# A one-core HGRN2/conv encoder layer: keys of six half heads made in a stage of their own and kept in DRAM

## The chip, the cores and the metric

One Trainium2 chip, one of its cores. The metric is device time in microseconds of one execution of the whole layer. Engines are named as in the profile: PE (matrix products), PEld (loading of a product's stationary operand), DVE (elementwise on vectors), ACT (activations, copies and casts), POOL, SP (which here only issues DMAs).

## The reference

One layer of a bidirectional encoder on 1024 positions x 1024 channels, float32 in and out:

```python
proj = jnp.einsum("bsd,de->bse", h, w_in)            # h = RMSNorm(x)
glu_in, q, v, z_f, z_b, og, g_a, g_b = jnp.split(proj, SPLIT_POINTS, axis=-1)
a = jax.nn.glu(glu_in, axis=-1)
a = _dwconv_centred(a, dw_w, dw_b)                   # 31 taps
a = jax.nn.silu(_layernorm(a, ln_w, ln_b))
a = jnp.einsum("bsc,cd->bsd", a, pw_w)               # the pointwise product
o = _bi_hgrn2(q, v, z_f, z_b, lb[0], lb[1])          # the scan, 8 heads of 128
of = o * lax.rsqrt(jnp.mean(o * o, axis=-1, keepdims=True) + EPS)
bmix = (of * norm_w * jax.nn.silu(og)) @ o_w
merged = jax.nn.sigmoid(g_a) * a + jax.nn.sigmoid(g_b) * bmix
...
# the scan, for each head and direction:
f = lb + (1.0 - lb) * jax.nn.sigmoid(z)              # decay, clipped to [1e-6, 1]
k = (1.0 - lb) * jax.nn.sigmoid(-z)
# S_t = diag(f_t) S_{t-1} + k_t v_t^T ,  o_t = S_t^T q_t
```

Then x += merged @ w_out, a gated FFN (up projection of 2 x 2816 columns, a 3-tap convolution on the gate, down projection), and a last RMSNorm.

## The kernel before

Activations lie with channels on the 128 partitions and positions along the row, in pages of 128x512 (a half of the positions; `H` is 512). A float32 product is made as three products of reduced operands (`mm3`, L138): an operand is split into a rounded part, an ACT cast (L121), and what is left, a subtraction on DVE or POOL (L118).

**Jobs and filler.** A job is the product of one block of 128 weight columns with all activations (`std_job`, L192), or a Strassen-like pair of blocks (`pair_job`, L224, whose weight sums are made by accumulating DMAs that POOL issues, L238). `run_jobs` (L149) prepares the weights of the next job, by an SP load into `wr`, an ACT cast and a DVE subtraction into `wp`, once the job before has begun. A job yields after every two steps of k, that is after six matmuls of 128x512: this is one unit. `Stream.fill(n)` (L172) advances a stream of jobs by n units, with the fraction carried over, so that units can be laid between other work. PE's instructions stand in the order in which the program issues them. The other engines' orders are made by the framework's scheduler from dependences and its own estimates.

**Order of the stages.** Input projection in 17 pairs, with the convolution beside it; layer norm of the convolved channels, for each half of the positions, after which the eight pointwise jobs of this half (2 units each, kept in the list `pw_jobs`) are put at the head of the list of jobs; then the scan, with 22 columns of the projection that are left over (`rest_jobs`, 176 units) as its filler stream `dense`; output projection of the scan, merge, w_out, FFN up, FFN down.

**The scan** has 16 half heads (8 heads, two halves of the positions; loop at L1011 to L1043). For half head i:

- `scan_inputs(i)` (L741) loads q and, for both directions, z, and makes on ACT the gates f and k (six activations), which DVE then clips (L762).
- `scan_base` (L765) is a generator: on DVE it makes products of decays within blocks of 8 positions (tile `DE`, with a reciprocal, L786), the block products `fm` and `tb`, the decayed queries and keys `Qh` and `Kh`, and from these `qF` and `kG`, which are what the levels start from. It yields between its instructions. One `Base` object holds the generator of the next half head, and is advanced by `step(BASE_STEPS)`, 2 yields.
- `scan_levels` (L825) makes the scores in four levels of block size 8, 16, 32 and 64. A level is an ACT copy of a part of kG to `A` (L835), four products of 128x128 (L838; the trace shows eight records), an update of kG (DVE, L730), a masked copy out of the bank (L865 to L869) and an update of qF; the next level needs both updates. The first level also has the products of Qh and Kh (L851).
- `scan_states` (L887) transposes kG (PE, L894), copies it out (`kT`, ACT, L896), multiplies by v and adds up the states `Sf` and `Sb`. The outputs of a head (L926 and L985) are made during the next head as the stream `pending`.

`between(fill)` (L1022) stands behind each of the four levels and the three steps of the states, seven times per half head: `dense.fill(FILL)` with FILL = 1.3, two steps of the next half head's keys, one step of `pending`. Before the first half head `dense.fill(21)` covers the making of its keys. Behind the last, `left` units (10) are laid between the last head's outputs and the loads of `bm` (L1001), the scan's results, which come back from DRAM for the output projection.

**Down projection.** 22 blocks of the FFN's hidden channels in groups of 4, 4, 5, 5, 4; for each group eight jobs. The pages of the next group are loaded and split (`load_g`) at once, three units into the group.

Of the kernel before, what the change touches and what calls it, by code (L numbers as in the profile page):

```python
# [10 lines left out]
F32 = mybir.dt.float32  # L11
# [5 lines left out]
AX = mybir.AxisListType  # L17

P = 128
FILL = 1.3  # L20
CONV_FILL = 1.6
NPAIRS = 17
LN_FILL = 6
# [21 lines left out]
def tile_hybrid_encoder(  # L45
# [45 lines left out]
    def nm(s):  # L91
        uid[0] += 1
        return f"{s}_{uid[0]}"
# [216 lines left out]
    ones_m = cp.tile([P, P], F32, name="ones_m")  # L310
    G.memset(ones_m, 1.0)

    gp0 = tc.alloc_tile_pool(name="gp0", bufs=1, reuse_waits="tile")
    p0 = tc.alloc_tile_pool(name="p0", bufs=1, reuse_waits="tile")
    x_in = []

# [346 lines left out]
    for half in range(2):  # L663
        xs = []
        for j in range(NCW):
            if j % 2 == 0:
                both = p1.tile([P, 2, H], F32, tag="ca", name=nm("cx"), bufs=2)
            nc.sync.dma_start(both[:, j % 2, :], d_cv[j][half])
            xs.append(both[:, j % 2, :])
        s_pairs.fill(LN_FILL)  # L670
        mean = bank("ob")
        T.matmul(mean, ones_m, total(xs, tmp()), start=True, stop=True)
        for t in xs:
            V.scalar_tensor_tensor(t, mean, -1.0 / CW, t, op0=ALU.mult, op1=ALU.add)
        s_pairs.fill(LN_FILL)
        sqs = [tmp() for _ in xs]
        for sq, t in zip(sqs, xs):
            A.activation(sq, t, AF.Square)
        rstd = rstd_over_partitions(total(sqs, sqs[0]), CW, "ob", tmp())
        next(rstd)  # L680
        s_pairs.fill(3)
        rs = next(rstd)
        ca = []
        for j, xn in enumerate(xs):
            V.tensor_tensor(xn, xn, rs, op=ALU.mult)
            V.tensor_scalar(xn, xn, vec("lnw", j), vec("lnb", j), op0=ALU.mult, op1=ALU.add)
            A.activation(xn, xn, AF.Silu)
            both = gp0.tile([P, 2, H], F32R, tag="gl", name=nm("ch"), bufs=NCW)
            ca.append(split(both[:, 0, :], both[:, 1, :], xn, V))
        s_pairs.fill(LN_LAST)  # L690
        at = 0
        while at < len(jobs) and jobs[at] in pw_jobs:
            at += 1
        for i in range(ND):
            job = std_job(
                w_cols(conv_pw_w, 0, NCW, i * P), NCW, lambda k, hf, ca=ca: ca[k], store(d_a[i]), (half,)
            )
            pw_jobs.append(job)
# [19 lines left out]
    hp = tc.alloc_tile_pool(name="heads", bufs=1, reuse_waits="tile")  # L718
    NB = H // 8
    DE = hp.tile([P, 2, 2, H], F32, name="DE")  # L720
    dg = hp.tile([P, H], F32, name="dg")
    E0, D0 = 0, 2 * H
    for o in (E0 + 3, D0 + 3):
        G.memset(view(DE, o, [[8, 2 * NB]]), 1.0)
    G.memset(dg, 0.0)

    N2 = 2 * NB

# [12 lines left out]
    def scan_inputs(i):  # L741


        h, half = divmod(i, 2)
        q = page(hp, "q", 2)
        f = hp.tile([P, 2, H], F32, tag="f", name=nm("f"), bufs=2)
        kk = hp.tile([P, 2, H], F32, tag="k", name=nm("k"), bufs=2)
        nc.sync.dma_start(q, d_q[h][half])
        for d in range(2):
            z = page(hp, "zi", 3)  # L750
# [4 lines left out]
            A.activation(  # L755
                fo,
                z.rearrange("p (b e) -> p b e", e=8),
                AF.Identity,
                scale=oml_of(d, h),
                bias=lb_of(d, h),  # L760
            )
        V.tensor_scalar(f, f, MIN_FORGET, 1.0, op0=ALU.max, op1=ALU.min)  # L762
        return q, f, kk, kscale[:, h : h + NH + 1 : NH]

    def scan_base(ins):  # L765


        q, f, kk, ks = ins

        def two(t, *r):  # L770
            if len(r) == 1:
                return view(t, r[0], [[8, N2]])
            return view(t, r[0], [[r[1] - r[0], 2], [8, N2]])

# [11 lines left out]
        V.reciprocal(ed(D, 7), ed(0, D + 7))  # L786
        yield

        fm = hp.tile([P, 2, NB], F32, tag="fm", name=nm("fm"), bufs=2)
        turned = view(fm, NB, [[-NB, 2], [1, NB]])  # L790
        tt(turned, view(f, 0, [[H, 2], [8, NB]]), view(DE, E0, [[H, 2], [8, NB]]))
        tb = hp.tile([P, 3, NB], F32, tag="tb", name=nm("tb"), bufs=3)
        tt(tb[:, 0:2, :], turned, view(DE, D + 7, [[H, 2], [8, NB]]))
        V.tensor_copy(tb[:, 2, :], tb[:, 0, :])
# [6 lines left out]
        qF = hp.tile([P, 2, H], F32, tag="qF", name=nm("qF"), bufs=3)  # L801
        kG = hp.tile([P, 2, H], F32, tag="kG", name=nm("kG"), bufs=2)
        Qh = hp.tile([P, 2, H], F32, tag="Qh", name=nm("Qh"), bufs=1)
        Kh = hp.tile([P, 2, H], F32, tag="Kh", name=nm("Kh"), bufs=1)
        along = [[8, NB], [1, 8]]
        for d in range(2):
            m0, st = ((0, 1), (7, -1))[d]
            whole = [[8, NB], [st, 8]]
            tt(view(Qh, (1 - d) * H + m0, whole), view(q, m0, whole), view(DE, D + d * H, along))
            yield  # L810
            keys(
                view(Kh, d * H + m0, whole),
                view(kk, d * H + m0, whole),
                ks[:, d : d + 1],
                view(DE, d * H, along),
            )
# [6 lines left out]
        yield qF, kG, [(Qh[:, 1 - d, :], Kh[:, d, :]) for d in range(2)], tb  # L823

    def scan_levels(base, S_t, Tt):  # L825

# [144 lines left out]

    class Base:
        def __init__(self, ins):
            self.gen, self.val = scan_base(ins), None

        def step(self, n):
            while n > 0 and self.val is None:
# [26 lines left out]
            bm[h][half] = split(hx(), hx(), load(d_bm[h][half]), V)  # L1004

    NI = 2 * NH
    cur = Base(scan_inputs(0))
    ins = scan_inputs(1)
    dense.fill(21)
    pending = Stream(iter(()))  # L1010
    for h in range(NH):  # L1011
        Tt = hp.tile([P, 2, 2, 4], F32, tag="Tt", name=nm("Tt"), bufs=3)
# [3 lines left out]
        for half in range(2):  # L1016
            i = 2 * h + half
            base = cur.result()
            ahead = Base(ins) if i + 1 < NI else None
            ins = scan_inputs(i + 2) if i + 2 < NI else None  # L1020

            def between(fill):  # L1022
                dense.fill(fill)
                if ahead is not None:
                    ahead.step(BASE_STEPS)
                pending.fill(1)

            S_t = hp.tile([P, 4, P], F32, tag="S", name=nm("S"), bufs=3)
            vl = load(d_v[h][half])
            for n, _ in enumerate(scan_levels(base, S_t, Tt[:, half])):  # L1030
                if n == 2:
                    b = bank("tr")
                    for c in range(4):
                        T.transpose(b[:, c * P : (c + 1) * P], vl[:, c * P : (c + 1) * P], ident)
                    v = hp.tile([P, 4, DK], F32, tag="v", name=nm("v"), bufs=3)
                    A.copy(v.rearrange("p c e -> p (c e)"), b)
                between(FILL)
            qF, kG = base[0], base[1]
            for _ in scan_states(i, kG, v, Tt, Sf, Sb):
                between(FILL)  # L1040
# [15 lines left out]
    bm_loads(1)  # L1056
    pending.drain()
    hp.release()


    fw = tc.alloc_tile_pool(name="fw", bufs=1, reuse_waits="tile")
# [310 lines left out]
```

## Time and profile before

| what | value |
|---|---|
| time, median of 3 runs | 1899.92 us (1898.41 to 1903.82) |
| the profiled execution | 1905.6 us, its span 1903.8 us |
| PE busy | 1799.7 us, 95% of the span |
| DVE, ACT, POOL busy | 67%, 42%, 11% |
| first level of the scan starts (PE, L838) | 561.15 us |
| first matmul of the output projection | 1011.00 us |
| q0 and q1 (the two queues with nearly all bytes), share of 16 engines | 15.2% and 41.5% |

The page has one profiled execution. A group or timeline line names line, engine, operation, output tile, input tile and shape; the bracket tells how long the engine was idle before and what ended it.

### The profile page before, as it was taken

The numbers are of one execution on the slowest core, as the hardware profiler recorded it, in microseconds if no ns is written. First come the engines' busy times: TensorE is split into PE (matmuls) and PEld (weight loads), VectorE is DVE, ScalarE is ACT, GpSimd is POOL, SyncE is SP. The second block draws the span as 40 slices with busy tenths as digits, with TensorE's granted clock in tenths as the row PEclk, the third lists the DMA queues.
The fourth block names the chain that finished last, engine by engine and source line by source line (L and its number), as shares of the span: only waits on it lengthen the run. The fifth ranks groups of instructions, "written<-read, shape, count | busy, mean of one in ns | idle before, by whom it ended". The sixth has DMA issues, their size and how long they took to land.

```text
span 1903.8 us, 23750 instructions
## 1 busy us (share of the span) xinstructions
PE 1799.7 (95%) x8543; PEld 1484.0 (78%) x8543; DVE 1270.2 (67%) x1860; ACT 799.2 (42%) x1488; POOL 210.9 (11%) x218
## 2 busy tenths in 40 slices
PE   6988999999999998999998999899999999999996
PEld 5767878887778887888786888588888888788885
DVE  3488999535469898999835555667676666534445
ACT  6433333234554554555443134544343344522124
POOL 3101111213100001000100000111111111000000
PEclk9999999999999999999998999899999999999998
DMA  7747788786563333342237665777676676733134
GB/s 256 219 119 169 179 188 199 185 182 148 190 192 89 113 108 96 111 122 82 75 95 216 197 200 183 185 153 154 147 151 143 143 156 128 221 93 96 54 89 162
DMA packets 323916, 285.09 MB, mean 150 GB/s; under 512 B 14926, under 2 KB 245078, under 8 KB 323798
## 3 DMA queue, kind: packets, MB, share of 16 engines
q1 hardware_dynamic: 272006, 242.67, 41.5%
q0 software_dynamic: 51792, 40.90, 15.2%
q8 instruction: 67, 1.10, 0.3%
q14 instruction: 51, 0.42, 0.1%
HBM read 191.24 MB, written 71.83 MB: 138 GB/s over the span
## 4 chain that ended last, share of the span: by engine, by line
PE 66%; DVE 13%; DMA 8%; ACT 6%; issue 3%; POOL 2%; SPq 0%; ACTq 0%; POOLq 0%; DVEq 0%
PE mm L143 16%; PE mm L144 16%; PE mm L145 16%; PE sc L144 3%; PE sc L145 3%; PE sc L143 3%; PE tr L143 2%; PE tr L144 2%; PE tr L145 2%; DVE wp L118 1%; DVE kG L730 1%; DVE DE L730 1%; PE sc L838 1%; DVE qF L730 1%; DMA wr<-wr 1%
## 5 line engine op out<-in xcount | busy, mean ns | idle before, releaser
L143 PE MATMUL mm<-hx,wp 128*128 128x512 f32 x1176 | 482.6, 410 | 24.6 <-ACT hx L121 8.6
L145 PE MATMUL mm<-hx,wp 128*128 128x512 f32 x1176 | 467.4, 397 | 3.9 <-DVE wp L118 3.9
L144 PE MATMUL mm<-hx,wp 128*128 128x512 f32 x1176 | 466.8, 397 | 2.9 <-POOL hx L118 1.9
L121 ACT CAST wp<-wr 128x1024 fp32r<-128x1024 f32 (+2 forms) x196 | 179.7, 917 | 323.0 <-PE mm L144 222.9
L143 PEld LDWEIGHTS mm<-hx,wp 128*128 128x128 f32 x1176 | 226.5, 193 | 73.7 <-ACT hx L121 9.5
L118 DVE TENSOR_TENSOR wp<-wr,wp 128x1024 fp32r<-128x1024 f32 (+2 forms) x196 | 206.9, 1056 | 102.9 <-ACT wp L121 97.4
L145 PEld LDWEIGHTS mm<-hx,wp 128*128 128x128 f32 x1176 | 225.5, 192 | 55.1 <-DVE wp L118 5.4
L144 PEld LDWEIGHTS mm<-hx,wp 128*128 128x128 f32 x1176 | 226.5, 193 | 48.4 <-POOL hx L118 3.6
L645 DVE SCALAR_TENSOR_TENSOR acc<-gl,v_b,acc 128x1024 f32<-128x1024 f32 x120 | 150.1, 1285 | 0.5
L143 PE MATMUL sc<-hy,wq 128*128 128x512 f32 x244 | 97.3, 399 | 3.1 <-ACT hy L121 3.0
L144 PE MATMUL sc<-hy,wq 128*128 128x512 f32 x244 | 96.7, 396 | 2.7 <-DVE hy L118 2.7
L145 PE MATMUL sc<-hy,wq 128*128 128x512 f32 x244 | 96.2, 394 | 0.0
L238 POOL DMA_DIRECT2D wr<-sw x39 | 34.9, 896 | 519.3 <-DVE wp L118 297.4
L1251 DVE TENSOR_TENSOR xr<-mm,xr 128x512 f32<-128x512 f32 x48 | 33.1, 690 | 82.0 <-PE mm L145 82.0
L838 PEld LDWEIGHTS sc<-qF,A 128*128 128x128 f32 x512 | 65.9, 193 | 19.0 <-issue 13.3
L838 PE MATMUL sc<-qF,A 128*128 128x128 f32 x512 | 69.1, 278 | 11.7 <-DVE qF L730 10.6
L121 ACT CAST wq<-sw 128x1024 fp32r<-128x1024 f32 x39 | 41.1, 1054 | 86.6 <-PE mm L144 66.4
L143 PE MATMUL mm<-hy,wp 128*128 128x512 f32 x156 | 63.2, 405 | 7.4 <-ACT wp L121 5.3
L266 ACT COPY su<-mm 128x512 f32<-128x512 f32 x78 | 45.5, 583 | 53.4 <-PE mm L145 53.4
L835 ACT COPY A<-kG 128x512 f32<-128x512 f32 x64 | 39.7, 620 | 66.3 <-DVE kG L730 37.8
L1169 DVE SCALAR_TENSOR_TENSOR tm<-gp,v_a,tm 128x512 f32<-128x512 f32 x88 | 65.6, 746 | 1.8 <-ACT tm L1165 0.9
L1153 DVE TENSOR_TENSOR ft<-su,mm 128x512 f32<-128x512 f32 x22 | 15.1, 687 | 71.6 <-issue 68.1
(281 smaller groups left out, 3548.6 us busy)
## 6 DMA issues: line engine op xcount, KB each, us to landing
wr<-in_w_in_dram SPq DMA_DIRECT2D x55, 512.0 KB, 6.5
sw<-in_ffn_w_up_dram SPq DMA_DIRECT2D x44, 256.0 KB, 3.5
sw<-in_ffn_w_up_dram POOLq DMA_DIRECT2D x22, 512.0 KB, 8.3
wr<-in_ffn_w_up_dram SPq DMA_DIRECT2D x22, 512.0 KB
d_g<-ft SPq DMA_DIRECT2D x44, 256.0 KB, 5.9
ev<-d_g SPq DMA_DIRECT2D x44, 256.0 KB, 3.2
wr<-sw POOLq DMA_DIRECT2D x39, 256.0 KB, 3.3
wr<-wr POOLq DMA_DIRECT2D x39, 256.0 KB, 3.8
```

The costliest lines, as they stand in the source:

```text
L118: eng.tensor_tensor(lo, src, hi.bitcast(F32), op=ALU.subtract)
L121: A.copy(hi, src)
L143: T.matmul(acc, whi[:, k, :], ahi, start=first, stop=False, skip_group_check=again)
L144: T.matmul(acc, whi[:, k, :], alo, start=False, stop=False, skip_group_check=again)
L145: T.matmul(acc, wlo[:, k, :], ahi, start=False, stop=last, skip_group_check=again)
L238: G.dma_start(o, a, accum_op=ALU.add)
L266: A.copy(t, acc)
L645: V.scalar_tensor_tensor(acc, g[:, k : k + S], tap(k), acc, op0=ALU.mult, op1=ALU.add)
L730: V.tensor_tensor(o, a, b, op=op)
L835: A.copy(A_t.rearrange("p (b x e) -> p b x e", x=2, e=h), pairs(kG, h))
L838: T.matmul(b[:, c * P : (c + 1) * P].rearrange("p (b x e) -> p b x e", x=2, e=h), A_t[:, c * P : (c + 1) * P], view(qF, c * P, [[2 * h, P ...
L1169: V.scalar_tensor_tensor(c, g[:, o + k : o + k + H], vec("fdw", k * NF + j), c, op0=ALU.mult, op1=ALU.add,)
```

## The change

- `EARLY = 6`. The eight pointwise jobs of the second half of the positions are no longer put at the head of the jobs ahead of the scan, but at the head of `dense`, which so has 192 units.
- A new stage stands between the projection and the scan: for half heads 0 to 5, `store_keys` makes inputs and keys (without qF and kG) into one page `Qk` of 128x2496 float32 (1.28 MB: Qh, Kh, fm, tb, and `ends`, a copy on ACT of the last decays of the blocks), and SP stores it to `d_keys[i]`. `Qk` has one buffer. At each of the nine yields of a half head one unit of `dense` is laid (54), and after the stage six more.
- In the scan, half heads 0 to 5 load their `Qk` back with one DMA and make only qF and kG (`scan_decayed`). The others make their keys as before, in the same page.
- The filler per slot is `EARLY_FILL` = 0.6 while the next half head is an early one, and FILL = 1.25 from then on. 15 units are left behind the last half head.
- The tiles of the gates lie in a pool of their own (`hb`), made before the stage, and the pool of the scan is made after it; the pool with the split convolution channels (`gp0`) is moved to the other side of the memory and lives until the keys are stored.
- In the down projection the loads and splits of the next group are spread: nine units, then one block of channels each four units.

```diff
-FILL = 1.3
+EARLY = 6
+EARLY_FILL = 0.6
+FILL = 1.25
...
+    KEYS = 4 * H + 7 * (H // 8)
+    d_keys = [dp.tile([P, KEYS], F32, name=f"d_keys_{i}") for i in range(EARLY)]
...
             pw_jobs.append(job)
-            jobs.insert(at + i, job)
+            if half == 0:
+                jobs.insert(at + i, job)
     s_pairs.drain()
     Stream(run_jobs(jobs)).drain()
     p1.release()
-    gp0.release()
...
-    dense = Stream(run_jobs(rest_jobs))
+    dense = Stream(run_jobs(pw_jobs[ND:] + rest_jobs))
...
+    def key_page():
+        t = hb.tile([P, KEYS], F32, tag="Qk", name=nm("Qk"), bufs=1)
+        Qh, Kh = t[:, 0 : 2 * H], t[:, 2 * H : 4 * H]
+        o = 4 * H
+        return t, Qh, Kh, t[:, o : o + N2], t[:, o + N2 : o + N2 + 3 * NB], t[:, o + N2 + 3 * NB :]
 
-    def scan_base(ins):
+    def scan_keys(ins, keyed):
         q, f, kk, ks = ins
+        t, Qh, Kh, fm, tb, ends = keyed
...
+    def scan_decayed(keyed, ends, along):
+        t, Qh, Kh, fm, tb, _ = keyed
+        qF = hp.tile([P, 2, H], F32, tag="qF", name=nm("qF"), bufs=3)
+        kG = hp.tile([P, 2, H], F32, tag="kG", name=nm("kG"), bufs=2)
         both = [[H, 2], [8, NB], [1, 8]]
         tt(view(qF, 0, both), view(Qh, 0, both), view(fm, 0, [[NB, 2], [1, NB], [0, 8]]))
         yield
-        tt(view(kG, 0, both), view(Kh, 0, both), view(DE, D + 7, [[H, 2], [8, NB], [0, 8]]))
+        tt(view(kG, 0, both), view(Kh, 0, both), view(ends, 0, along + [[0, 8]]))
         yield
...
+    def store_keys(i):
+        keyed = key_page()
+        yield from scan_keys(scan_inputs(i), keyed)
+        A.copy(view(keyed[5], 0, [[NB, 2], [1, NB]]), ends_of())
+        nc.sync.dma_start(d_keys[i], keyed[0])
+
+    def scan_base(i, ins):
+        keyed = key_page()
+        if i < EARLY:
+            nc.sync.dma_start(keyed[0], d_keys[i])
+            yield
+            yield
+            yield from scan_decayed(keyed, keyed[5], [[NB, 2], [1, NB]])
+        else:
+            yield from scan_keys(ins, keyed)
+            yield from scan_decayed(keyed, DE[:, 1, 0, 7:], [[H, 2], [8, NB]])
...
-    cur = Base(scan_inputs(0))
-    ins = scan_inputs(1)
-    dense.fill(21)
+    for i in range(EARLY):
+        for _ in store_keys(i):
+            dense.fill(1)
+    gp0.release()
+    hp = tc.alloc_tile_pool(name="heads", bufs=1, reuse_waits="tile")
...
+    def inputs(i):
+        return i, scan_inputs(i) if i >= EARLY else None
+
+    cur = Base(inputs(0))
+    ins = inputs(1)
+    dense.fill(6)
...
-                between(FILL)
+                between(FILL if i + 1 >= EARLY else EARLY_FILL)
...
-    left = 8 * (len(rest) - 2) + 16 - dense.count
+    left = 2 * ND + 8 * (len(rest) - 2) + 16 - dense.count
...
             if not last:
-                load_g(f0 + group, groups[n + 1])
+                st.fill(9)
+                for f in range(f0 + group, f0 + group + groups[n + 1]):
+                    load_g(f, 1)
+                    st.fill(4)
             st.drain()
```

More of the change, by code (lines that the diff above doesn't have):

```diff
@@ L311, in tile_hybrid_encoder @@
     G.memset(ones_m, 1.0)
-    gp0 = tc.alloc_tile_pool(name="gp0", bufs=1, reuse_waits="tile")
+    gp0 = tc.alloc_tile_pool(name="gp0", bufs=1, side="right", reuse_waits="tile")
     p0 = tc.alloc_tile_pool(name="p0", bufs=1, reuse_waits="tile")
@@ L714, in tile_hybrid_encoder @@
         h12.append(split(hx(), hx(), t, V))
-    dense = Stream(run_jobs(rest_jobs))
-    hp = tc.alloc_tile_pool(name="heads", bufs=1, reuse_waits="tile")
+    dense = Stream(run_jobs(pw_jobs[ND:] + rest_jobs))
+    hb = tc.alloc_tile_pool(name="gates", bufs=1, reuse_waits="tile")
     NB = H // 8
-    DE = hp.tile([P, 2, 2, H], F32, name="DE")
-    dg = hp.tile([P, H], F32, name="dg")
+    DE = hb.tile([P, 2, 2, H], F32, name="DE")
     E0, D0 = 0, 2 * H
@@ L744, in scan_inputs @@
         h, half = divmod(i, 2)
-        q = page(hp, "q", 2)
-        f = hp.tile([P, 2, H], F32, tag="f", name=nm("f"), bufs=2)
-        kk = hp.tile([P, 2, H], F32, tag="k", name=nm("k"), bufs=2)
+        q = page(hb, "q", 2)
+        f = hb.tile([P, 2, H], F32, tag="f", name=nm("f"), bufs=2)
+        kk = hb.tile([P, 2, H], F32, tag="k", name=nm("k"), bufs=2)
         nc.sync.dma_start(q, d_q[h][half])
         for d in range(2):
-            z = page(hp, "zi", 3)
+            z = page(hb, "zi", 3)
             nc.sync.dma_start(z, d_z[d][h][half])
@@ L787, in scan_base @@
         yield
-        fm = hp.tile([P, 2, NB], F32, tag="fm", name=nm("fm"), bufs=2)
         turned = view(fm, NB, [[-NB, 2], [1, NB]])
         tt(turned, view(f, 0, [[H, 2], [8, NB]]), view(DE, E0, [[H, 2], [8, NB]]))
-        tb = hp.tile([P, 3, NB], F32, tag="tb", name=nm("tb"), bufs=3)
-        tt(tb[:, 0:2, :], turned, view(DE, D + 7, [[H, 2], [8, NB]]))
-        V.tensor_copy(tb[:, 2, :], tb[:, 0, :])
+        tt(view(tb, 0, [[NB, 2], [1, NB]]), turned, view(DE, D + 7, [[H, 2], [8, NB]]))
+        V.tensor_copy(tb[:, 2 * NB :], tb[:, 0:NB])
         tt(ed(D + 1, 6), ed(D, 7), fv(1, 7))
@@ L799, in scan_base @@
         yield
[L801 to L804, printed above, removed]
         along = [[8, NB], [1, 8]]
@@ L820, in scan_base, with ends_of @@
         yield
-        tt(view(kG, 0, both), view(Kh, 0, both), view(DE, D + 7, [[H, 2], [8, NB], [0, 8]]))
+        tt(view(kG, 0, both), view(Kh, 0, both), view(ends, 0, along + [[0, 8]]))
         yield
-        yield qF, kG, [(Qh[:, 1 - d, :], Kh[:, d, :]) for d in range(2)], tb
+        qk = [(Qh[:, (1 - d) * H : (2 - d) * H], Kh[:, d * H : (d + 1) * H]) for d in range(2)]
+        yield qF, kG, qk, tb
+    def ends_of():
+        return view(DE, D0 + 7, [[H, 2], [8, NB]])
+    def store_keys(i):
[13 more added lines that the diff above has]
+            yield from scan_decayed(keyed, DE[:, 1, 0, 7:], [[H, 2], [8, NB]])
     def scan_levels(base, S_t, Tt):
@@ L973, in __init__ @@
         def __init__(self, ins):
-            self.gen, self.val = scan_base(ins), None
+            self.gen, self.val = scan_base(*ins), None
         def step(self, n):
@@ L1006, in tile_hybrid_encoder @@
     NI = 2 * NH
-    cur = Base(scan_inputs(0))
-    ins = scan_inputs(1)
-    dense.fill(21)
+    for i in range(EARLY):
[3 more added lines that the diff above has]
+    hp = tc.alloc_tile_pool(name="heads", bufs=1, reuse_waits="tile")
+    dg = hp.tile([P, H], F32, name="dg")
+    G.memset(dg, 0.0)
+    def inputs(i):
[3 more added lines that the diff above has]
+    dense.fill(6)
     pending = Stream(iter(()))
@@ L1019, in tile_hybrid_encoder @@
             ahead = Base(ins) if i + 1 < NI else None
-            ins = scan_inputs(i + 2) if i + 2 < NI else None
+            ins = inputs(i + 2) if i + 2 < NI else None
             def between(fill):
@@ L1036, in tile_hybrid_encoder @@
                     A.copy(v.rearrange("p c e -> p (c e)"), b)
-                between(FILL)
+                between(FILL if i + 1 >= EARLY else EARLY_FILL)
             qF, kG = base[0], base[1]
             for _ in scan_states(i, kG, v, Tt, Sf, Sb):
-                between(FILL)
+                between(FILL if i + 1 >= EARLY else EARLY_FILL)
             kept.append((S_t, v, qF))
@@ L1058, in tile_hybrid_encoder @@
     hp.release()
+    hb.release()
     fw = tc.alloc_tile_pool(name="fw", bufs=1, reuse_waits="tile")
```

1 line of the change is left out of this document (removed).

## The prediction

> **What bounds the kernel now.** I read the shares of the page, then the stretch around the scan as windows (columns: length, busy us and instructions of PE, weight load, DVE, ACT, POOL; granted clock, DMA share, GB/s): two parts of the projection ahead of the scan, half heads 0 to 5, half heads 6 to 15, and the way into the output projection.
>
> ```profile
> PE 1799.7 (95%) x8543; PEld 1484.0 (78%) x8543; DVE 1270.2 (67%) x1860; ACT 799.2 (42%) x1488; POOL 210.9 (11%) x218
> ```
>
> ```profile
> 507.90:532.50 24.60, 23.19 (x97) 18.04 (x97) 8.57 (x12) 10.83 (x19) 0.00 (x0) 1.00 0.67 202
> 532.50:561.10 28.60, 28.60 (x127) 23.62 (x126) 17.82 (x28) 17.61 (x28) 1.08 (x3) 1.00 0.65 201
> 561.10:715.60 154.50, 142.43 (x885) 124.87 (x885) 143.78 (x263) 82.56 (x179) 6.77 (x8) 0.98 0.34 105
> 715.60:976.60 261.00, 244.65 (x1562) 214.56 (x1562) 225.11 (x420) 135.43 (x318) 19.97 (x20) 0.99 0.31 96
> 976.60:1016.60 40.00, 28.70 (x140) 23.43 (x139) 13.37 (x22) 17.81 (x45) 4.03 (x5) 0.86 0.49 135
> ```
>
> PE is full except in the scan and behind it, and the change leaves PE's instructions as many as they were: it can only move PE's waits. At full rate a 512-wide matmul starts every 0.227 us (560.24, 560.46, 560.69) and a 128-wide one every 0.112. The first six half heads hold 324 wide and 561 narrow ones: 136.4 us of 154.5, so 18.1 are lost; the other ten 546 and 1016: 237.7 of 261.0, 23.3 lost. DVE is busy 93% of the first six. The idle time of PE from 561 to 1017, by what ended it (us, times, longest):
>
> ```profile
> PE sc L838 <- DVE qF L730: 10.6, 9, 2.8
> PE mm L143 <- ACT hx L121: 8.3, 1, 8.3
> PE tr L894 <- ACT kT L896: 7.4, 3, 2.9
> ```
>
> The second row is one gap, at the first output projection job; PE's and ACT's timelines show it (start, length, instruction, idle before it and its releaser):
>
> ```profile
> 571.74 2.05 PE L838 MATMUL sc<-qF,A 128*128 128x128 f32 x8 [2.78 <-DVE qF L730]
> ...
> 1007.43 1.04 ACT L121 CAST wq<-sw 128x1024 fp32r<-128x1024 f32 x1 [7.88 <-DMA sw<-in_ffn_w_up_dram]
> ...
> 1011.00 0.79 PE L143 MATMUL mm<-hx,wp 128*128 128x512 f32 x1 [8.27 <-ACT hx L121]
> ```
>
> ACT stands in a cast of the first FFN weight, whose transfer POOL issued at 996.66, with the hx splits behind it. Gaps of over 2.5 us are followed by slow PE: the level at 571.74 takes 2.05 us where the one at 561.15 takes 1.05, and behind a 4.61 us gap at 1644.65 twelve matmuls start 0.44 apart (a further 2.5 us).
>
> **A. The key stage and the way into the scan.** DVE's timeline prices one half head's keys:
>
> ```profile
> 544.20 0.69 DVE L762 TENSOR_SCALAR f<-f 128x1024 f32<-128x1024 f32 x1 [9.04 <-ACT f L755]
> ...
> 547.22 1.75 DVE L786 RECIPROCAL DE<-DE 128x256 f32<-128x256 f32 x1
> ...
> 555.26 0.74 DVE L733 SCALAR_TENSOR_TENSOR Kh<-k,kscale,DE 128x512 f32<-128x512 f32 x1
> 555.92 1.22 DVE L730 TENSOR_TENSOR qF<-Qh,fm 128x1024 f32<-128x1024 f32 x1
> 557.05 1.22 DVE L730 TENSOR_TENSOR kG<-Kh,DE 128x1024 f32<-128x1024 f32 x1
> ```
>
> From 544.20 to 549.78 it is 5.6, then 0.1 for a copy and 4.0 from 551.62 to 555.92 less the strips between: 9.7 us, and 2.4 more for qF and kG, which stay in the scan. PE now runs 54 filler units (6 wide matmuls, 1.36 us each) plus 6 from 507.9 on, 23 of them after where the first level starts today: with no wait the scan would begin at 561.15 + 23 x 1.36 = 592.5. DVE sets another pace. The first f is clipped near 521 (the first pointwise job is out by 515, then a table load and six activations, about 5 us). Its keys take 9.7 and four weight splits of the pointwise jobs 0.6 each: 532.7. In the order of the built program the weight cast of the first other job stands on ACT behind the copy of the ends, which waits for those keys; with cast 1.05 and subtract 1.2 it is ready at 537.1, where PE would have it at 532.3: a wait of 4.8. Half heads 1 to 5 take 9.7 + 1.2 for a split, 10.9, up to 12.5 each with the waits for f. At 12.5 the last keys are done at 595, PE's units at 597.3.
>
> Then the new round trip: Qk has one buffer, so load 0 waits for store 5. A 256 KB page is stored in 2.2 and loaded in 2.9 us (d_z and zi of the issue table), at 2048 B packets of 84 ns on 16 engines 0.7 of it transfer; 1.278 MB makes it 3.3: store 4.8, load 5.4. With the copy 0.3, issue 0.8, qF and kG 2.4 and the A copy 0.8 the first level follows the last keys by 14.5 us: 609.6, so PE, out of units at 597.3, waits 12.3. Two slow restarts of 2.5 bring the stage to 4.8 + 12.3 + 5 = 22.1. With pace 10.9 the keys end 8 us earlier (587): level at 601.6, 9.1 behind 592.5, with one restart 11.6. If nothing at all waits but the round trip, less the 7 units that stand behind the last key step (9.5), it is 14.4 - 9.5 + 2.5 = 7.4. If DMA stretches the stage (below) 34. I take the middle of 11.6 and 22.1: **+17**, bounds 7.4 and 34.
>
> The 18 loads of q and z of these half heads leave SP earlier, the 12 key transfers (15.3 MB) are new. They stand in SP's queue with the weight loads of the jobs, which run one job (10.9 us) ahead; a load held 5 us behind a store that waits for its keys is still early. The DMA engines were at 0.67 share there: this is the cover, and if it is gone the next rival's price holds. POOL gets nothing new here.
>
> **B. Half heads 0 to 5.** DVE loses 9.7 of its some 25 us in each, PE 0.7 x 7 = 4.9 filler units. What then bounds is the chain from level to level. At the end of the scan, where there is no filler, it shows itself:
>
> ```profile
> 961.00 0.74 DVE L869 COPY_PREDICATED S<-m,sc 128x512 f32<-128x512 uint8 x1 [0.49 <-PE sc L838]
> 961.65 0.66 DVE L730 TENSOR_TENSOR qF<-qF,tb 128x512 f32<-128x512 f32 x1
> ```
>
> From the last product of a level to the next level PE waits 1.7 us (a copy .74, a qF .67, latency), of which a unit covers 1.36 and transposes of v .36. With 0.6 units a slot, about every other slot has none. Walking the built PE order with these prices, the six wait 3.3, 2.1, 2.7, 2.5, 2.0 and 2.3, and the 2 to 3 clock drops of such gaps cost 0.45 each per half head: 17.6, against 18.1 lost now. **-0.5**; bounds -11 (all six lose the 1.2 of the best half heads, 10 and 11) and +6 (all like today's third, 4.7 us, with half again for the load of Qk).
>
> **C. Half heads 6 to 15.** FILL 1.25 for 1.3 takes 3.5 units (4.8 us) from a stretch where DVE bounds about half of the slots (the second of each pair of half heads waits 1.3 to 2): they come back behind the scan as PE work. **+2.4**; bounds 0 and 4.8.
>
> **D. The way out of the scan.** Today 976.6 to 1017 loses 1.4 (Sb), 0.7, 8.3, 1.0 and 2.5 of slow PE: 13.8. Five more units are left (15 for 10), 6.8 us in which the FFN weight can come; and the built order has POOL's transfer ahead of the last head's rstd and ACT's cast of it in the last half head, ahead of its kT copies. There ACT's cast waits 10.8 us from issue (996.66 to 1007.43): kT comes at 20.7 us into the half head where PE wants it at 16.0, 4.7 and a restart of 2.5. Two loads of bm at a time (988.63, 993.97, 999.42: 5.4 us a round) still cost 3. -13.8 + 4.7 + 2.5 + 3 = **-3.6**; bounds -13.8 and +3 (the cast waits as long as today, in the scan, and the bm round twice).
>
> **E. Down projection.** With the d_g loads spread one f at a time, ACT's splits stand less in front of the xr copies, which end the 4.61 gap at 1644.65: **-1.3**, a guess at one split and its share of the restart; bounds -4.5 (the gap gone) and 0, since no load moves ahead of what it fed before.
>
> Sum: 17 - 0.5 + 2.4 - 3.6 - 1.3 = +14.0. It is a difference between stretches of one execution (span 1903.8, reported 1905.6, 5.7 above the median of 1899.92), and I put it on the median: 1913.9.
>
> The slow restart by row is 2.5 us. The Trainium skill (TensorE: Matmul & The Clock Gate, Part 1: The HAM clock gate) says that an idle PE falls to half clock and needs about 3.4 us of sustained work to come back; half of 3.4 is 1.7 a restart, an estimate from that page, and with it the sum would be 1.2 lower (one or two restarts in A). The trace gives more (2.5), and I keep it.
>
> **Rivals.** Faster: the first level starts within some 5 us of the last filler unit (A 7.4), early half heads, freed of 39% of their DVE work, lose like the best (B -11), and the last half head has its FFN weight in time (D -12): 7.4 - 11 + 2.4 - 12 - 1.3 = -14.5, 1885.4. For it: DVE at 93%, and 10.6 us of waits for qF. Against: units are fewer exactly where the chain, not DVE's sum, is the wait. It decides if the levels find qF ready with 0.6 units a slot. Chance 0.22.
>
> Slower still: the stage is bound by DMA. Per half head of 11.6 us it moves a stored Qk (1.28 MB), three loaded pages (0.79) and one job's weights and stores (1.05 per 10.9 us, so 1.12): 3.19 MB, 275 GB/s; 202 at share 0.67 scales to 301, so 0.91 of what there is. Stores then take 8 us for 4.8 and, with one Qk, DVE stands 2.5 us in each of five half heads: 12 to 17 more in A, 34 in all: 1930.9. Against: the mean leaves room. Chance 0.12. The Trainium skill (DMA: Bandwidth & Descriptors, Specifications) names 358 GB/s per core from HBM; by that the stage would be at 0.77, and this rival weaker.
>
> No change: A 11.6, B -0.5, C 2.4, D -10, E -1.3: +2.2, 1902.1; for it, the tail's 8.3 us gap has a plain cause that is moved. Chance 0.13. That the change doesn't do what it says is excluded by the built order: six sets of keys and stores stand ahead of the first level, six loads behind.
>
> **How the numbers follow.** The forecast has 0.53. Its own range is 1903 to 1924 (A 11.6 to 22.1, the rest by half its bounds). 8 in 10: from 1889, cutting half of the faster case, to 1928, cutting most of the DMA case. 0.3%, 5.7 us, is what a measurement can tell: faster 0.23 (that rival, and a sliver of the third), same 0.12, slower 0.65 (forecast and DMA case).
>
> **What would show it.** A: a PE gap of some 12 us ahead of the first level, ended by DVE's qF behind a load of Qk; about 5 at the first job after the pointwise ones, ended by DVE's wp. B: half heads 0 to 5 lose some 3 us each as now. D: no 8 us gap at the output projection, and an ACT cast in the last half head that waits on sw with PE behind it for kT. Wrong would be: the first level within 5 us of the last unit, half heads 0 to 5 at under 1.5 lost, or stores of Qk over 8 us.

## The result, and the profile after

The changed kernel takes 1910.55 us (median of 20 runs, 1899.45 to 1919.86) against 1901.24 us for the kernel before beside it (20 runs, 1897.0 to 1911.81): 1.0045 of its time, 95% interval 1.003 to 1.006, so 6 to 11 us slower. In a second series (12 runs, and 34 of the kernel before) the ratio was 1.0039 (1.0025 to 1.0053). The forecast was 14 us more.

The runs of one kernel lie up to 20 us apart here. The profiled execution of the changed kernel (1899.45 us) is the fastest of its 20, and that of the kernel before (1905.6 us) one of the slower: the two pages compared as wholes would say that the change gains 6 us. So the stretches are compared, over several profiles, and the sums are checked against medians. One source of the scatter, found in e3, bears on every comparison here.

Page of the changed kernel, the engines' shares, and its windows (columns as in the prediction): the key stage, the wait behind it, half heads 0 to 5, half heads 6 to 15, the way out.

```profile
PE 1792.4 (94%) x8543; PEld 1478.2 (78%) x8543; DVE 1277.0 (67%) x1860; ACT 802.2 (42%) x1494; POOL 208.0 (11%) x218
```

```profile
532.00:592.00 60.00, 59.44 (x261) 48.73 (x261) 55.62 (x87) 32.54 (x54) 0.00 (x0) 1.00 0.84 283
592.00:605.30 13.30, 0.76 (x5) 0.30 (x3) 5.35 (x9) 2.70 (x5) 0.00 (x0) 0.68 0.79 266
605.30:727.97 122.67, 110.42 (x734) 98.56 (x735) 97.24 (x177) 58.98 (x139) 5.58 (x8) 0.97 0.35 114
727.97:981.97 254.00, 238.67 (x1538) 210.07 (x1537) 224.63 (x420) 133.91 (x316) 18.58 (x21) 0.99 0.33 100
981.97:1022.00 40.03, 38.73 (x194) 31.79 (x193) 14.27 (x23) 20.15 (x48) 2.42 (x4) 1.00 0.53 163
```

PE is full in the key stage (59.4 of 60 us, at 283 GB/s), idle for 12.5 us behind it, and full again behind the scan (38.7 of 40.0, where it was 28.7). DVE, at 93% in the first six half heads before, is at 79% there now. PE's idle time from 555 to 1017 us, by what ended it:

```profile
PE sc L871 <- ACT A L868: 12.5, 1, 12.5
PE sc L871 <- DVE qF L732: 10.4, 11, 1.5
PE tr L927 <- DVE ev L998: 8.9, 7, 2.7
```

The 8.3 us at the output projection are gone; 12.5 us at the first level have come; the waits for qF are what they were (10.6 before), though DVE has less to do. The long gap in the timelines of SP, DVE and PE:

```profile
588.80 0.38 SPq L844 DMA_DIRECT2D d_keys<-Qk  x1
594.89 0.32 SPq L850 DMA_DIRECT2D Qk<-d_keys  x1
...
602.23 1.23 DVE L732 TENSOR_TENSOR qF<-Qk 128x1024 f32<-128x1024 f32 x1 [7.85 <-DMA Qk<-d_keys]
...
605.29 2.08 PE L871 MATMUL sc<-qF,A 128*128 128x128 f32 x8 [12.54 <-ACT A L868]
```

Behind the last keys (588.54) come a store of 6 us, only then the load into the same buffer, 7.3 us to qF, then kG and A. The last filler unit has started by 592.4. The way out of the scan, ACT's and PE's timelines:

```profile
976.45 1.05 ACT L123 CAST wq<-sw 128x1024 fp32r<-128x1024 f32 x1 [6.46 <-DMA sw<-in_ffn_w_up_dram]
...
979.92 1.16 PE L936 MATMUL ob<-v,kT 128*128 128x128 f32 x8 [1.84 <-ACT kT L929]
```

ACT waits for the FFN weight in the last half head, ahead of the kT copies, and PE waits for these, but for 1.8 us.

### The profile page after: what moved, and what is told of

Same layout as the page of the kernel before. It is cut to its first block, busy times and chain, and to the rows that moved or that the text cites. A ratio compares the mean times of both kernels' runs of the same rounds, so it can differ in the third digit from the quotient of the medians.

```text
span 1897.7 us, 23788 instructions
## 1 busy us (share of the span) xinstructions
PE 1792.4 (94%) x8543; PEld 1478.2 (78%) x8543; DVE 1277.0 (67%) x1860; ACT 802.2 (42%) x1494; POOL 208.0 (11%) x218
## 4 chain that ended last, share of the span: by engine, by line
PE 59%; DVE 16%; DMA 13%; ACT 6%; issue 4%; POOL 1%; SPq 1%; ACTq 0%; POOLq 0%; DVEq 0%
PE mm L145 14%; PE mm L146 14%; PE mm L147 14%; PE sc L146 3%; PE sc L147 2%; PE sc L145 2%; DMA sw<-in_w_in_dram 2%; DMA wr<-wr 2%; DMA wr<-sw 2%; DVE DE L732 2%; DVE wp L120 2%; DMA sw<-in_ffn_w_up_dram 1%; PE sc L871 1%; DVE Qk L732 1%; DVE acc L649 1%
## 5 line engine op out<-in xcount | busy, mean ns | idle before, releaser
L145 PE MATMUL mm<-hx,wp 128*128 128x512 f32 x1176 | 476.2, 405 | 14.4 <-ACT wp L123 4.4
L147 PE MATMUL mm<-hx,wp 128*128 128x512 f32 x1176 | 463.7, 394 | 3.8 <-DVE wp L120 3.8
L146 PE MATMUL mm<-hx,wp 128*128 128x512 f32 x1176 | 462.5, 393 | 2.1 <-POOL hx L120 1.8
L145 PEld LDWEIGHTS mm<-hx,wp 128*128 128x128 f32 x1176 | 223.3, 190 | 62.7 <-DVE ev L592 5.4
L147 PEld LDWEIGHTS mm<-hx,wp 128*128 128x128 f32 x1176 | 222.7, 189 | 54.7 <-DVE wp L120 6.7
L146 PEld LDWEIGHTS mm<-hx,wp 128*128 128x128 f32 x1176 | 223.5, 190 | 47.6 <-POOL hx L120 3.6
L871 PE MATMUL sc<-qF,A 128*128 128x128 f32 x512 | 69.4, 279 | 23.0 <-ACT A L868 12.5
L123 ACT CAST wq<-sw 128x1024 fp32r<-128x1024 f32 x39 | 41.1, 1054 | 84.8 <-PE mm L146 66.9
L145 PE MATMUL mm<-hy,wp 128*128 128x512 f32 x156 | 63.2, 405 | 6.7 <-ACT wp L123 5.3
L147 PE MATMUL mm<-hy,wp 128*128 128x512 f32 x156 | 62.6, 401 | 0.0
```

Of the source, the lines that this page charges most:

```text
L123: A.copy(hi, src)
L145: T.matmul(acc, whi[:, k, :], ahi, start=first, stop=False, skip_group_check=again)
L146: T.matmul(acc, whi[:, k, :], alo, start=False, stop=False, skip_group_check=again)
L147: T.matmul(acc, wlo[:, k, :], ahi, start=False, stop=last, skip_group_check=again)
L871: T.matmul(b[:, c * P : (c + 1) * P].rearrange("p (b x e) -> p b x e", x=2, e=h), A_t[:, c * P : (c + 1) * P], view(qF, c * P, [[2 * h, P ...
```

## The experiments

Each kernel was timed in five rounds beside the kernel before, except e11. "Loss" is PE's time in a half head less its work at full rate (0.227 us for a wide, 0.112 for a narrow matmul).

**e1: the changed kernel again.** No edit.

> The changed kernel once more, to see which of its waits are the same in a second profiled execution. Theory (the sum of the prediction): the one long gap of PE ahead of the first level is 12 to 13 us again, no gap over 4 us stands between the scan and the output projection, and the time is 8 to 10 us above the kernel before. Rival (the time beyond the first profile, which came out 11 us under the median, lies in the change): some gap that the first profile doesn't have, of 5 us or more, stands in the key stage, the scan or the down projection.

1904.55 us, ratio 1.0039 (7.4 us over before). The gap ahead of the first level is 10.9 us and starts the level at 605.63 (605.29 in the first profile); no gap over 2.8 us stands between it and the output projection. Nothing new in the second profile, and yet an execution 5 us longer: the first profile was a lucky execution of the same mechanism, as the theory says, though the gap is a little under its 12 to 13.

**e2: half head 0 stays in Qk.**

```diff
-    for i in range(EARLY):
+    for i in [*range(1, EARLY), 0]:
         for _ in store_keys(i):
...
-        nc.sync.dma_start(d_keys[i], keyed[0])
+        if i:
+            nc.sync.dma_start(d_keys[i], keyed[0])
+        else:
+            in_place.append(keyed)
...
-        keyed = key_page()
+        keyed = key_page() if i else in_place.pop()
         if i < EARLY:
-            nc.sync.dma_start(keyed[0], d_keys[i])
+            if i:
+                nc.sync.dma_start(keyed[0], d_keys[i])
```

> The keys of half heads 1 to 5 are made first, those of half head 0 last; these stay in Qk and are neither stored nor loaded. All else as in the changed kernel. Theory (the first level waits for the store of the last keys and the load of the first, one behind the other on one buffer): the 12.5 us gap of PE at the first level is gone or under 2.5 us, and the time is 12 to 15 us under the changed kernel's (1896 to 1899). Rival (the stage is late because DVE's keys are late, or because DMA is full): the gap shrinks by less than half, to 6 us or more, the time by less than 6 us. Second rival: the gap moves to half head 1, whose load now waits for Qk to be free of half head 0: the levels of half head 1 start 5 us later and half of the gain is lost.

1895.65 us, ratio 0.9987 (0.997 to 1.0004); the changed kernel beside it 1904.55. PE's timeline at the first level:

```profile
593.54 0.39 PE L147 MATMUL mm<-hx,wp 128*128 128x512 f32 x1
593.76 1.05 PE L875 MATMUL sc<-qF,A 128*128 128x128 f32 x8
```

There is no gap at all, and the level starts 11.9 us earlier than in e1 (11.5 earlier than in the first profile); a 2.1 us gap opens at the second level. So the round trip is the wait. The gain, 8.9 us between the medians, is less than the 12 to 15 expected, and half head 1 is not late (2.75 lost, 2.76 before this edit), so the second rival falls.

**e3 and e4: the spread loads of the down projection.** e3 takes them out of the changed kernel, e4 puts them alone into the kernel before.

```diff
-                st.fill(9)
-                for f in range(f0 + group, f0 + group + groups[n + 1]):
-                    load_g(f, 1)
-                    st.fill(4)
+                load_g(f0 + group, groups[n + 1])
```

> The changed kernel with the loads and splits of the next group of the down projection at once, as before the change; the rest of the change stays. Theory (the spread is worth what the profiles differ by behind 1632 us, 5 us): 4 to 6 us slower than the changed kernel, 1914 to 1917, and a gap of PE over 4 us at the start of the down projection. Rival (what the prediction took, one split less ahead of the xr copies): 1 to 2 us slower.

> The kernel before with the spread loads of the down projection alone. Theory: 4 to 6 us faster than the kernel before, 1895 to 1897, the 4.6 us gap at the start of the down projection under 3 us. Rival: 1 to 2 us faster, 1899 to 1900, the gap nearly as long.

e3: 1906.78 us, ratio 1.0051 (1.0033 to 1.007), 2.2 us over e1. e4: ratio 0.9991 (0.9973 to 1.0008), about 1.7 us under before, not clear of nothing. The gap at the start of the down projection is 4.15 us in e3, 2.85 in e4. On the gap both theories came true (over 4 us, under 3), on the time their rival: what the prediction had taken (1.3) is nearer, and the 5 us between the first two profiles were scatter.

e3 also showed one place where scatter comes from. Its code differs from e1's only behind 1600 us, but its half head 12 lost 9.2 us, in e1 1.9. POOL's timeline, e3 first and then e1:

```profile
898.76 7.32 POOL L409 TENSOR_TENSOR ors<-ors,mhalf 128x4 f32<-128x4 f32 x1
```

```profile
895.35 1.01 POOL L409 TENSOR_TENSOR ors<-ors,mhalf 128x4 f32<-128x4 f32 x1
```

The same instruction, the root of four numbers per partition, takes 1.01 us in one execution and 7.32 in another. ACT's scaling of the outputs waits for it, and PE for that.

**e5 and e8: FILL alone, and with the spread loads,** in the kernel before.

```diff
-FILL = 1.3
+FILL = 1.25
```

> The kernel before with FILL 1.25 instead of 1.3 and nothing else, so that 15 units are left behind the scan. Theory (the 8 us gap at the output projection is ACT's wait for the first FFN weight, and what removes it in the changed kernel is where the cast stands and the five more units, not the keys): the gap is under 3 us, the time 6 to 10 us under the kernel before, the losses of the half heads as before. Rival (it takes the earlier place in the last half head, which only the changed kernel's order has): a gap of 5 us or more stays and the time is within 4 us of the kernel before.

> The kernel before with FILL 1.25 and the spread loads of the down projection, without early keys: the two parts of the change that should gain. Theory (parts add up): 8 to 11 us under the kernel before, and so 15 or more under the changed kernel. Rival (both stages end in a wait that takes the place of the one removed): within 4 us of the kernel before.

Ratios 1.0002 (0.9987 to 1.0018) and 1.0 (0.9981 to 1.0018): no gain. But the gap at the output projection is 1.5 us in both, where the kernel before and e4 have 8.3 and 7.5. So the theory of the tail is right, the time is not. In both, half head 4 loses 12.5 and 12.8 us, in the kernel before 2.7, and POOL's, ACT's and PE's timelines of e5 say why:

```profile
671.55 5.46 POOL L405 TENSOR_TENSOR ors<-ors,mhalf 128x4 f32<-128x4 f32 x1
...
677.04 1.28 ACT L955 ACTIVATE tm<-tm,ors 128x128 f32<-128x128 f32 x4 [6.65 <-POOL ors L405]
...
686.84 1.11 PE L894 MATMUL tr<-ident,kG 128*128 128x128 f32 x4 [6.30 <-ACT kT L896]
```

With other filler the instructions of the half heads shift against each other, and the long POOL operation turns up at another head: what the tail gained was given back there. e8 has it at the same place (5.49 us).

**e6 and e7: more filler in the early half heads,** on e2's kernel.

```diff
-EARLY_FILL = 0.6
-FILL = 1.25
+EARLY_FILL = 1.3
+FILL = 1.0
...
-    dense.fill(6)
+    dense.fill(3)
```

e7 has 1.0 and 1.1 in place of 1.3 and 1.0.

> The kernel with half head 0 in place (run before), with 1.3 filler units per slot in half heads 0 to 4, 1.0 in the later ones and 3 units for 6 ahead of the scan. Theory (with 0.6 units a slot the wait is the chain from level to level, not DVE's sum): half heads 0 to 4 lose under 8 us of PE together, where they lose 18 with 0.6; half heads 6 to 15, where DVE bounds, lose 1 to 2 us more each than with 1.25, so that the time is 0 to 8 us above the same kernel with 0.6 and 1.25. Rival (what PE waits for in the early half heads is not a matter of filler: ACT's copies, the root of the outputs on POOL): they still lose 14 us or more.

> The same with 1.0 in half heads 0 to 4, 1.1 later and 3 units ahead of the scan. Theory: half heads 0 to 4 lose about 10 us, 6 to 15 some 0.5 us more each than with 1.25; the time is 3 us under to 2 us above the kernel with half head 0 in place. Rival (the loss has nothing to do with filler): half heads 0 to 4 lose 14 us or more, the time is 4 us or more above it.

e6: ratio 1.0023 (1.0009 to 1.0037), by the ratios 7 us over e2. Half heads 0 to 4 lose 5.7 us together, with 0.6 units 18.4 (e2); half heads 6 to 15 lose 41.1, where e2 loses 20.3. The rival falls: with keys ready ahead, it is filler that covers the chain of the levels. In the late half heads more than the expected 1 to 2 us each are lost, 6.8, 9.7, 6.6 and 3.9 in half heads 8, 10, 12 and 14. Not all of that is filler. POOL's timeline has, at half head 10, the operation ahead of the root, which takes 0.19 us when DVE is idle:

```profile
847.18 5.61 POOL L408 TENSOR_SCALAR ors<-oss 128x4 f32<-128x4 f32 x1 [42.93 <-ACT jk L985]
```

In half heads 12 and 14 no such operation is over 1.4 us, so the missing units are the likelier cause there; the two were not separated.

e7: ratio 1.0112 (1.0086 to 1.0138), 21 us over before, which no theory expected. Half heads 0 to 4 lose 13.3 us, half heads 8, 10, 12 and 14 lose 8.7, 8.5, 8.4 and 7.7. POOL's, DVE's and ACT's timelines at the first of these:

```profile
789.57 5.21 POOL L409 TENSOR_TENSOR ors<-ors,mhalf 128x4 f32<-128x4 f32 x1
...
790.02 1.22 DVE L732 TENSOR_TENSOR qF<-Qk 128x1024 f32<-128x1024 f32 x1
791.15 1.22 DVE L732 TENSOR_TENSOR kG<-Qk,DE 128x1024 f32<-128x1024 f32 x1
792.29 0.68 DVE L732 TENSOR_TENSOR qF<-qF,tb 128x512 f32<-128x512 f32 x1
...
794.50 0.39 DVE L732 TENSOR_TENSOR DE<-DE,f 128x128 f32<-128x128 f32 x1
796.67 0.75 DVE L1002 SCALAR_TENSOR_TENSOR ev<-tr,v_a,tm 128x512 f32<-128x512 f32 x1 [1.78 <-PE tr L1000]
...
794.82 1.28 ACT L992 ACTIVATE tm<-tm,ors 128x128 f32<-128x128 f32 x4 [6.43 <-POOL ors L409]
```

DVE runs one operation behind another, nearly all with two inputs in SBUF; POOL's ends at 794.78, just before DVE's last of the row ends (794.89). DVE then has nothing to do, because the chain waits for POOL.

**e11: e7's kernel once more,** one profiled execution, not timed in rounds. The label says otherwise; the root is in this kernel.

> A second profile of the kernel with half head 0 in place and 1.0 and 1.1 units per slot. Theory (the long POOL operations belong to this order of instructions, where DVE leaves no pause at that place): the operations near 790, 845, 900 and 955 us take over 4 us again and half heads 8, 10, 12 and 14 lose over 7 us each. Rival (chance of one execution): at least two of them take under 2 us.

The four operations take 5.21, 5.24, 5.85 and 4.38 us at 794, 849, 904 and 961 us, and the half heads lose 8.8, 8.5, 11.2 and 7.7. So in this order they are no chance of one execution; in e3 against e1 they were.

**e9 and e10: the root left out,** in the changed kernel and in the kernel before.

```diff
-            rstd_small(rs, ss, DK)
+            A.activation(rs, ss, AF.Copy, scale=1.0 / DK)
```

> The changed kernel without the root of the output normalisation in the scan (L408 and L409, two small operations on POOL per half): ACT multiplies the sums of squares by 1/128 instead, so the root itself is left out. Theory (POOL's 128x4 operations, 1.0 us when free, wait for DVE wherever DVE runs two-input operations one behind another, up to 7.3 us, and PE and ACT wait with them): half heads 6, 8, 12 lose 1 to 4 us less, the time is 3 to 7 us under the changed kernel, and its runs spread less than the 12 to 20 us seen so far. Rival (those waits are hidden, the spread has another source): within 2 us of the changed kernel, the spread as wide.

> The same in the kernel before, the root left out. Theory: half heads 2, 6, 12 and 14, which lose 31.9 us with e4's profile counted (4.8, 6.1, 8.0, 3.7) and 17 in the first profile, lose under 8 together; the time is 6 to 12 us under the kernel before. With it the changed kernel's loss against before, both without the root, is 9 to 14 us: the change's own cost, apart from POOL. Rival: within 2 us of the kernel before.

e9: 1892.4 us, ratio 0.997 (0.9956 to 0.9984) to the kernel before. e10: 1877.92 us, ratio 0.9899 (0.988 to 0.9918). So leaving out the two small POOL operations is worth 19 us in the kernel before and some 14 in the changed kernel (0.997 against 1.0039 to 1.0045), both more than expected. Without the root the changed kernel is 0.7% slower (0.997 by 0.9899), 13 to 14 us. The runs of e9 spread over 8.5 us, those of e10 over 6.2; but e5 and e6, with the root in, spread over 7.9 and 9.3, so the spread does not show where the scatter comes from.

Half heads 2, 6, 12 and 14 of e10 lose 1.80, 0.42, 1.54 and 0.12 us, under 8 together as expected. (The 31.9 in the expectation is a slip: its four numbers add up to 22.6.) Half heads 6, 8 and 12 of e9 lose about 1.7, 2.9 and 0.4 us less than in the first profile of the changed kernel.

The edit does two things: it ends the long POOL operations, and it takes POOL's 1.2 us (0.19 and 1.01) out of the chain even where they are short. Both count. From the first profile of before to e10, half heads 2, 4, 6 and 14, where POOL has operations of 1.4 to 4.0 us, lose 14.7 us less, and half heads 8 to 12, where none is over 1.4, lose as much as before: there the short operations are hidden. But half heads 2 and 8 of the changed kernel lose 3.5 and 2.9 us less in e9, although no POOL operation there takes over 1.03 us in its first profile. So the 19 and 14 us are not all waiting for DVE, and how much of them is was not separated.

**e12: less filler in the last head only,** with the spread loads, no early keys.

```diff
-                between(FILL)
+                between(FILL if h < NH - 1 else 0.95)
```

> The kernel before with 0.95 units per slot in the last head alone (15 units left behind the scan, as in the change) and the spread loads of the down projection, no early keys; the other seven heads keep 1.3. Theory (the gain of the tail is real, and FILL 1.25 everywhere gave it back at another half head): 7 to 11 us under the kernel before, the gap at the output projection under 3 us, half heads 0 to 13 as in the kernel before. Rival (the tail gives it back itself, in the last head with less filler): within 4 us of the kernel before.

1883.77 us against 1898.12, ratio 0.9934 (0.9912 to 0.9957): 8 to 17 us faster than the kernel before (7 to 11 were expected), and the fastest kernel here that leaves nothing out. Its profile is the fastest of its six runs (1878.64 us). Windows of half heads 0 to 5, 6 to 15 and the 40 us behind them:

```profile
553.44:705.54 152.10, 141.17 (x886) 123.29 (x885) 143.30 (x262) 82.10 (x179) 6.01 (x8) 0.99 0.33 106
705.54:957.50 251.96, 237.92 (x1532) 209.24 (x1531) 224.10 (x417) 134.94 (x317) 17.06 (x20) 0.99 0.30 95
957.50:997.50 40.00, 36.41 (x171) 28.60 (x170) 14.45 (x25) 18.30 (x45) 3.97 (x5) 0.93 0.64 180
```

The gap at the output projection is 1.7 us (28.7 us of PE work in the 40 us were there before, 36.4 are now), half heads 0 to 13 keep the order of the kernel before, and the 5 us that half head 14 lost are 2.0. In the kernel before and in e4 a root of 4.0 us stands in that half head, in e12 none over 1.01; so a part of the gain may be the same shift of POOL's operations as in e5, this time a lucky one.

## Why the prediction was right, and where it was not

Slower was forecast, by 14 us; it is slower by 7 to 9. Term by term, as means over two profiles of before (with e4, the same up to the down projection) and three of after (with e1, and e3 up to there), from the first pointwise matmul of the second half to the first matmul of w_out:

| term | forecast | measured | without the root (e9 less e10) |
|---|---|---|---|
| A, key stage to first level | +17 | +18.0 | +19.0 |
| B, half heads 0 to 5 | -0.5 | +2.1 | +3.8 |
| C, half heads 6 to 15 | +2.4 | -1.6 | +2.0 |
| D, way out of the scan | -3.6 | -12.1 | -10.0 |
| E, down projection | -1.3 | about -2 (e3, e4) | |

A takes 23 units of 1.361 us off for the work that was moved, D adds the 6 units (8.2 us) that come later, by the matmuls counted in the half heads.

- **A was right in sum, and by its main mechanism** (e2). The gap behind the stage is 12.5, 10.9 and 14.1 us in the three profiles, where the prediction had 9.1 to 12.3. The round trip was dearer: 16.7 us from the last key to the level, for 14.5, at 283 GB/s and a DMA share of 0.84. DVE's pace (keys done at 576.99, 588.54) was 11.5, between its 10.9 and 12.5. The wait of 4.8 us at the first job after the pointwise ones did not come: the prediction had the copy of the ends wait for all keys, but it needs only the products in DE, and stood at 525.8, not behind 532.7. In its place PE waits at the fifth of the eight pointwise jobs, where ACT casts a job's weights only after the six activations of half head 0, and then runs slowly. ACT's and PE's timelines of the changed kernel:

```profile
514.86 1.50 ACT L757 ACTIVATE f<-zi,lbw 128x512 f32<-128x512 f32 x2
...
516.73 0.62 ACT L123 CAST wp<-wr 128x512 fp32r<-128x512 f32 x1
...
517.40 0.50 PE L145 MATMUL mm<-ch,wp 128*128 128x512 f32 x1 [1.94 <-ACT wp L123]
...
519.38 0.63 PE L145 MATMUL mm<-ch,wp 128*128 128x512 f32 x1
```

Ahead of the last unit PE loses 7.5 to 8.7 us in the three profiles, 2.2 and 2.8 in the two of before: 5.6 more, the size of the forecast wait and its restart, by another wait. The unhindered count's 592.5 for the last unit came true by chance, because the stage began 5.7 us earlier in this profile (502.28 for 507.95).
- **The slow restart** of 2.5 us was read from the row with the longest one. In the same profile PE loses 1.7 us behind gaps of 2.6, 3.4 and 2.7 us (at 20, 103 and 441 us), which is the prediction's other estimate.
- **B** had the right mechanism, the chain of the levels with too few units (e6), and half heads 0 to 5 lose 20.4 where the walk gave 17.6. What it missed is that some 5 of the 18.1 lost before go with POOL's root: without it the first six half heads lose 11.4 before and 15.2 after, so that the early keys cost 3.8 there. (1.8 more of the difference is in half head 0, which has no root, since a head's outputs are made during the next.) Its upper bound of +6 does not follow from its words: six half heads at 4.7 us lose 28.2, 10 more than 18.1.
- **C** comes out at the size forecast only without the root (+2.0). With it the long operations, 9.2 us lost in one half head of e3 and 8.0 in one of e4, outweigh the term.
- **D is the term that was mis-sized.** The cast that moved into the last half head does wait and PE does wait for kT behind it, but the transfer took 6.5 us (969.93 to 976.45) for the 10.8 taken from the row of before, so PE waits 1.8 us and has no restart where 7.2 stood; and the 3 us for the loads of bm are hidden by the units left over. The five units, not the keys, remove the old gap (e5, e12).
- **E** was about right.
- **The rival of a full DMA** falls: the stage ran at a share of 0.84 with PE busy for 59.4 of 60 us. The last store took 6.1 us and the first load 7.3, counted from issue, under the 8 that the prediction named as a sign, and DVE waits 0.33 us once for a store of Qk. The faster rival falls on the first level, which came 13 us behind the last unit, and on B.

The measured terms add up to 4.4 us, the times to 7 to 9. With the root left out they add up to 12.8 with E, the times to 13.5. The sum over profiles is off by about what POOL's operations vary between a few executions, two of before and three of after; that this is all of the rest was not shown. So the direction rests on A, which was understood, and the size owes something to luck: the other terms came out 2.6 us over and 4.0, 8.5 and 0.7 under the forecast, and their sum lies nearer to the +2.2 of the no-change case, whose D of -10 was the better one, than to 14.

That leaving out the root is worth 19 us before and 14 after, so that some 5 us of the change's own cost do not show in the times, is what the prediction did not see. It read the waits for ACT's tm, kT and DVE's ev as the end of a chain on these engines and did not ask why ACT was late.

The Trainium skill (SBUF — State Buffer, Who interferes with whom) says that DVE instructions with two SBUF inputs contend with a POOL instruction that reads SBUF. It calls the ports that the two share an exclusive lock, and says of DVE's two-port modes that whichever issues first has them for its whole instruction while the other blocks. In the twelve profiles with the root in, the trace agrees that the two get in each other's way: 39 root operations (L405 and L409) during which DVE was busy under a fifth of the time all take 1.01 to 1.03 us. Of 117 beside a DVE busy over 90% of the time the median is 1.03 but nine take over 3 us, and so do five of the 36 between. What the runs have beyond the page is that POOL can stay out over some ten DVE operations in a row. That the port is the reason was not tested by a run of its own, and why most operations beside an equally busy DVE are not held up stays open.

## What to carry to other kernels

Work stored away from one stage and loaded in the next needs its first piece in place: with one buffer the last store and the first load stand one behind the other, with nothing to hide them (a PE gap of 10.9 to 14.1 us here). Filler units move the cover, they do not make any: in e6 the early half heads gained 13 us by them, and the late ones lost 21, a part of it to a POOL operation that shifted. And before a few per cent are read out of one profile, look for the operation whose duration differs between two executions of the same code; an edit can lose or gain more by shifting it than by what it was made for.

## What the runs showed of the hardware

- A POOL operation on 128x4 numbers takes 1.01 us beside an idle DVE and 4.0 to 7.3 us at some places beside a DVE that runs operations, most of them with two inputs, with hardly a pause; one that takes 0.19 us took 5.61 (e6). Which ones are long depends on the order of instructions (e7 and e11: four times, at the same places), and at some places on the execution (half head 12 of the changed kernel: 1.0, 2.5 and 7.3 us in three executions whose code up to there is the same).
- PE gaps of the same length cost different amounts: half head 8 of the changed kernel has a gap of 2.71 us with a granted clock of 0.94 over the half head and a loss of 4.6 us, e2's has 2.72 us, a clock of 1.00 and 3.0.
